# Three reordered steps, no address pads and a few more buffers in a transformer-like block of three token mixers

## The chip, the cores and the metric

The kernel runs on one core of one Trainium2 chip. The metric is the device time of one execution in microseconds; lower is better. All times below are for that one core.

## The reference

One layer over 512 positions of width 1024, all in float32: an RMS norm, one input projection whose columns feed three token mixers and three gates, a merge with an output projection and a residual, and a SwiGLU FFN (inner width 2816) with a second residual.

```python
h = rms_norm(x, norm_mix)
u_pool, u_lru, q, k, v, g_logits = split(h @ w_in)
gates = sigmoid(g_logits + b_gate)                  # three of them
y_pool = pool_mixer(u_pool, w_pool, pool_scale)     # windows 2, 4, 8, 16: mean minus the token, a map per group
y_lru = rglru_mixer(u_lru, ...)                     # see below
y_sb = stick_breaking_attention(rms_norm(q), rms_norm(k), v)   # 8 heads of 128
merged = sum(gates[i] * (y_i @ w_branch[i]))
x = x + merged @ w_out
h2 = rms_norm(x, norm_ffn)
out = x + (silu(h2 @ w_ffn_gate) * (h2 @ w_ffn_up)) @ w_ffn_down

# rglru_mixer
xc = conv_b + sum(conv_w[k] * shifted(u, k))        # width 4, causal
r, i = sigmoid(xb @ w_rg + b_rg), sigmoid(xb @ w_ig + b_ig)    # block-diagonal
log_a = -8 * r * softplus(-lru_lambda)
a, mult = exp(log_a), sqrt(-expm1(2 * log_a))
h = scan(h_prev * a + mult * (i * xc))
```

## The kernel before, in words

**Numbers.** Every float32 product is made from two reduced-precision parts: an operand is split into a high part (ScalarE copies it to the matmul's type) and a low part (VectorE subtracts the high part from the original), and three matmuls are done, high by high, high by low and low by high. A weight tile is 128 partitions by 1024 values. `split_w` and `split_a` do the splits; the tiles `whi` and `wlo` come from a rotation of three buffers each, which `weight_tiles` hands out.

**Products.** Half of the products (`mm3`, `chan_chunk`) are plain, with 512 columns per matmul. The others (q, k, v, the third branch's gates and projection, most of the FFN) use a seven-product scheme of block matrices: the blocks "11", "12", "S2", "S1", "S3", "S4", "22" are sums and differences of quarter matrices. Most of these have 256 columns per matmul.

**Order.** The program is written out by hand, with one long list of weight tiles (`specs`) that `weights()` fetches, loads and splits ahead of use. Background work stands in lists (`bg`, `abg`); `tick()` takes one item off between groups of matmuls, and `step()` appends one. A scheduler then orders each engine's instructions by priority (earlier in the program is higher; `tc.high_priority(n)` raises it by n) and by when buffers and operands are ready. Each engine works through its own order strictly.

**Stages.** (1) The input norm and the first two branches' gates. (2) The recurrence in four chunks of 256 channels: `lru_chunk` does the projection, `conv`, `split` (`xch`, `xcl`) and the gates' matmuls `lg` with tanh on ScalarE; then `lru_exp`, `lru_decay`, `lru_input`, `lru_scan`, `lru_store`. `lru_exp` takes the exponentials in place in `r` and the square root of `t` into a new tile `ls`; `lru_decay` overwrites `t`. (3) The seven-products for v, k, q (tiles `ps_q`), then the third branch's gates (`ps_gx`, `ps_gy`, in two blocks `cc`), stored to DRAM. (4) The pooling mixer in four chunks (`pool_chunk`, in the order of `POOL`) with the attention heads as background. `evac_u` copies a finished pooling bank to a work buffer `up`, and `pool_mean` and `pool_back` go on from there. (5) The plain branch projections (`ps_br`) with loads of gates (`g`). (6) The third branch (`ps_bY`, `ps_bX`), the output projection (`ps_out`), the second norm. (7) The FFN: two chunks of 256 inner channels are plain ("direct", `ps_fg` and `ps_fu`, then `sg` and `act`), nine are seven-products (`seven(c)`, tiles `ps_y`, `ps_x`), and the down product (`ps_dy`, `ps_dx`) ends it.

**Buffers.** In the first stages the pool `ap0` has buffers of 4 KB per partition under three tags: "w" (8, for weights of the seven-products), "t" (8) and "b" (13). In the mixer stage `slot` hands out work buffers of 2 KB (NSP - NLD = 30) and `slot_ld` load buffers (NLD = 12), into which SyncE's queue loads three tiles `at` for each attention head and two gate tiles `g` for each chunk of a branch. `gp` in the FFN has GBUFS = 27 buffers.

**Pads.** `weight_tiles` makes tiles of 1024 + 128 values and uses 1024 of them from offset `o`. It is 0 in the plain products; in the seven-products of 256 columns the first four tiles of a stage take 0, 4, 8 and 12 (STEPS) and all later ones 16 (OFF). One more tile, `pad`, of 41 values stands near the start of memory.

Of the kernel before, what the change touches and what calls it, by code (L numbers as in the profile page):

```python
# [16 lines left out]
P = 128  # L17
# [11 lines left out]
GBUFS = 27  # L29
# [5 lines left out]
PAD = 41  # L35


OFF = 16
STEPS = (0, 4, 8, 12)
NAW, NAT, NAB = 8, 8, 13  # L40
NSP = 42
# [26 lines left out]
def layer_kernel(ctx: ExitStack, tc: tile.TileContext, x, xt, vecs, w_in, w_qkv7, w_gate7, w_pool, w_rg, w_ig,  # L68
# [65 lines left out]
    def split_w(raw, shape, n, o=0):  # L134
        hi, lo = weight_tiles("whi" + n, "wlo" + n, o)
        if len(shape) == 3:
            hi, lo = (t.rearrange("p (a b) -> p a b", a=shape[1]) for t in (hi, lo))
        else:
            hi, lo = (t.rearrange("p (a b c) -> p a b c", a=shape[1], b=shape[2]) for t in (hi, lo))
        with tc.high_priority(60):  # L140
            act(hi, raw, AF.Copy)  # L141
            dve.tensor_tensor(lo, raw, hi.bitcast(F32), ALU.subtract)  # L142
        return hi, lo
# [58 lines left out]
    def add_seven(un, nm, i):  # L202
        u, pieces, shape = UNITS[un]
        last = i == pieces - 1

        def make(n):
            if nm == "S4":
                r = qraw[u, "12", i]
                dve.tensor_tensor(r, r, qraw[u, "S2", i], ALU.add)
            src = qraw[u, {"S1": "21", "S3": "11", "S4": "12"}.get(nm, nm), i]  # L210
            o = 0
            if u >= 3:
                o = goffs.pop(0) if goffs else OFF
            parts = split_w(src, [P] + list(shape), n, o)
# [12 lines left out]
    goffs = list(STEPS)  # L227

# [29 lines left out]
    boffs = list(STEPS)  # L258
# [4 lines left out]
    def add_branch7(u, nm):  # L263
        def make(n):
# [5 lines left out]
            parts = split_w(t, [P, 2, 4, P], n, boffs.pop(0) if boffs else OFF)  # L270
# [58 lines left out]

    cst.tile([P, PAD], F32, tag="pad", name="pad")  # L330
    warm = cst.tile([P, S], BF16, tag="warm", name="warm")
# [109 lines left out]
    with ExitStack() as first:  # L441
# [12 lines left out]
        for i in range(WARM):  # L454
            nc.tensor.matmul(wps[:, 0, :], warm[:, 0:P], warm, start=True, stop=True)
# [233 lines left out]
        def lru_exp(cs):  # L689
            for c in cs:  # L690
                for j in range(2):
                    r = lru[c]["r"][:, j, :]
                    ct = 2 * c + j
                    act(r, r, AF.Exp, scale=cneg[:, ct:ct + 1], bias=cneg[:, ct:ct + 1])
            for c in cs:
                lru[c]["s"] = b4([2, S], f"ls{c}")
                act(lru[c]["s"], lru[c]["t"], AF.Sqrt, scale=0.25)


        def lru_decay(c):  # L700
            e, t = lru[c]["r"], lru[c]["t"]
            dve.scalar_tensor_tensor(t, e, 1.0, t, ALU.add, ALU.mult)
            if c < 2:
                dve.tensor_scalar(t, t, -1.0, 1.0, ALU.mult, ALU.add)
            else:
                act(t, t, AF.Identity, scale=-1.0, bias=1.0)

        def lru_input(c):
            e, s_ = lru[c]["r"], lru[c]["s"]
# [3 lines left out]
        def lru_scan(c):  # L713
            t, s_ = lru[c]["t"], lru[c]["s"]
# [62 lines left out]
        for f, c in ((lru_decay, 2), (lru_decay, 3), (lru_input, 2)):  # L777
            step(of(f, c))
# [112 lines left out]
        for cc in range(2):  # L891
            tx, ty = b4([2, S], f"gx{cc}"), b4([2, S], f"gy{cc}")
# [49 lines left out]
    with ExitStack() as mix:  # L942
# [35 lines left out]
        def evac_u(ps, name):  # L978
            u = slot(name)
            act(two(u), in_order(ps), AF.Copy)  # L980
# [314 lines left out]
    with ExitStack() as ffn:  # L1295
# [115 lines left out]
        offs = []  # L1411
# [14 lines left out]
        def make_a(upto):  # L1426
            while made[0] < min(upto, len(steps)):
                c, nm = steps[made[0]]
                made[0] += 1
                if (c, nm) == (NDIRECT, "11"):  # L1430
                    offs.extend(STEPS)
# [6 lines left out]
        def split_a(src, n):  # L1438
            o = offs.pop(0) if offs else OFF
            h, l = (t.rearrange("p (w k c) -> p w k c", w=2, k=4)  # L1440
                    for t in weight_tiles("wh" + n, "wl" + n, o))
# [35 lines left out]
        def seven(c):  # L1477
# [13 lines left out]
            for n, (nm, ps, half, first, t, ts_, src, ss) in enumerate(plan):  # L1491
# [8 lines left out]
                if nm == "22":  # L1500
                    finish_act(ty, Y, a[:, 1, :])
            acts.append(a)

        bg.extend([lambda: None, rms2] + prepare_b())
        for c in range(NDIRECT):
# [5 lines left out]
            for j in range(2):  # L1511
# [4 lines left out]
                dve.tensor_tensor(a[:, j, :], sg, rb2, ALU.mult)  # L1516
            acts.append(a)
        tick(len(bg))
        for c in range(NDIRECT, NF // 2):
# [49 lines left out]
        def make_d(upto):  # L1569
            while dmade[0] < min(upto, len(dsets)):  # L1570
                nm, n = dsets[dmade[0]]
                dmade[0] += 1
                if dmade[0] == 1:
                    offs.extend(STEPS)
# [157 lines left out]
```

## Time and profile before

| | us |
|---|---|
| median of 3 runs | 872.93 (872.79 to 872.95) |
| the profiled execution, its own time | 872.6 |
| its span from first to last instruction | 870.8 |
| TensorE busy | 859.7 |
| VectorE busy | 741.2 |
| ScalarE busy | 522.1 |
| granted TensorE clock, mean | 1.00 |

In the profile PE is TensorE's matmuls, PEld its weight loads, DVE is VectorE, ACT ScalarE, POOL GpSimd and SP SyncE; L123 is a line of the kernel before. A row of a timeline gives start, duration, engine, line, operation, the tile written and the tiles read, and in brackets how long the engine stood idle before it and what ended that. The end of a matmul is modelled, so two matmuls are compared by their starts. A row of the chain that ended last gives the start, the length and the work.

### The profile page before, as it was taken

How to read it: one execution, taken by the hardware profiler on the slowest of the kernel's cores; microseconds unless marked ns; L12 is line 12 of the kernel's file. 1: busy time of each engine (PE TensorE's matmuls, PEld its weight loads, DVE VectorE, ACT ScalarE, POOL GpSimd, SP SyncE). 2: the span in 40 equal slices, each digit the busy share in tenths (PEclk: the TensorE clock that was granted, in tenths of full speed). 3: DMA queues.
4: the chain of work that ended last, by engine and by line, in shares of the span. 5: the costliest groups of instructions: out<-in, count | busy, mean ns of one | idle time of the engine just before them, and what ended most of it. 6: DMA issues, size and time to landing. Idle time of an engine off the chain costs nothing.

```text
span 870.8 us, 14268 instructions
## 1 busy us (share of the span) xinstructions
PE 859.7 (99%) x5563; PEld 789.7 (91%) x5563; DVE 741.2 (85%) x961; ACT 522.1 (60%) x727; POOL 91.8 (11%) x130
## 2 busy tenths in 40 slices
PE   9999999999999999999999999999999999999998
PEld 7888878888899888889889998889999999999998
DVE  7899897998787699977898786699988888899974
ACT  6554989556856565565665545464555555755642
POOL 1110002232433101000001100000000000121200
PEclk9999999999999999999999999999999999999999
DMA  9686356799582786635736955345543343798913
GB/s 340 167 291 195 97 169 194 215 318 253 176 271 73 238 246 205 218 122 155 217 98 152 212 171 170 98 138 151 150 117 97 106 114 109 233 243 204 192 39 121
DMA packets 116643, 154.08 MB, mean 177 GB/s; under 512 B 8160, under 2 KB 90080, under 8 KB 116576
## 3 DMA queue, kind: packets, MB, share of 16 engines
q1 hardware_dynamic: 103904, 107.30, 38.5%
q0 software_dynamic: 12528, 45.62, 22.1%
q8 instruction: 43, 0.70, 0.3%
q10 hardware_dynamic: 144, 0.26, 0.1%
q14 instruction: 24, 0.20, 0.1%
HBM read 132.71 MB, written 18.87 MB: 174 GB/s over the span
## 4 chain that ended last, share of the span: by engine, by line
PE 76%; DVE 10%; ACT 6%; DMA 4%; issue 2%; SPq 1%; POOL 0%; ACTq 0%; DVEq 0%; POOLq 0%
PE ps_y L318 10%; PE ps_x L318 8%; PE ps_q L834 6%; PE ps_dy L1651 6%; PE ps_dx L1651 5%; DVE wlo L142 3%; PE ps_br L309 3%; PE ps_br L310 3%; PE ps_br L311 3%; PE ps_bY L1277 2%; PE ps_gate L737 2%; DMA qw<-in_w_gate_dram 2%; PE ps_bX L1277 2%; ACT whi L141 2%; PE ps_gy L318 2%
## 5 line engine op out<-in xcount | busy, mean ns | idle before, releaser
L141 ACT ACTIVATE whi<-raw 128x1024 fp32r<-128x1024 f32 x69 | 72.8, 1055 | 76.8 <-PE ps_out L310 16.0
L142 DVE TENSOR_TENSOR wlo<-raw,whi 128x1024 fp32r<-128x1024 f32 x69 | 84.2, 1220 | 23.6 <-ACT whi L141 23.0
L142 DVE TENSOR_TENSOR wlo<-qw,whi 128x1024 fp32r<-128x1024 f32 x48 | 58.4, 1219 | 17.3 <-ACT whi L141 17.1
L141 ACT ACTIVATE whi<-qw 128x1024 fp32r<-128x1024 f32 x48 | 50.4, 1052 | 29.9 <-PE ps_q L834 14.9
L1442 ACT ACTIVATE wh_S<-w_S 128x1024 fp32r<-128x1024 f32 x36 | 38.0, 1059 | 33.0 <-PE ps_y L318 19.9
L1555 POOL DMA_DIRECT2D dw<-in_w_down_dram x20 | 16.9, 862 | 306.3 <-DMA dw<-in_w_down_dram 263.8
L1443 DVE TENSOR_TENSOR wl_S<-w_S,wh_S 128x1024 fp32r<-128x1024 f32 x36 | 43.7, 1220 | 3.8 <-ACT wh_S L1442 3.8
L1442 ACT ACTIVATE wh<-w 128x1024 fp32r<-128x1024 f32 x27 | 28.6, 1058 | 26.9 <-issue 9.1
L1443 DVE TENSOR_TENSOR wl<-w,wh 128x1024 fp32r<-128x1024 f32 x27 | 32.9, 1220 | 8.4 <-ACT wh L1442 8.4
L1442 ACT ACTIVATE whdS<-dw 128x1024 fp32r<-128x1024 f32 x20 | 21.2, 1058 | 21.3 <-PE ps_dy L1651 10.6
L1443 DVE TENSOR_TENSOR wldS<-dw,whdS 128x1024 fp32r<-128x1024 f32 x20 | 24.2, 1220 | 5.5 <-ACT whdS L1442 5.5
L1093 DVE TENSOR_TENSOR_SCAN E<-K,ahead 128x512 f32<-128x512 f32 (+3 forms) x32 | 25.3, 812 | 3.9 <-ACT K L1089 3.9
L309 PE MATMUL ps_br<-yHH,whi 128*128 128x512 f32 x64 | 24.6, 385 | 1.4 <-ACT up L980 1.4
L309 PE MATMUL ps_lru<-HH,whi 128*128 128x512 f32 x64 | 24.6, 384 | 0.0
L309 PE MATMUL ps_br<-yph,whi 128*128 128x512 f32 x64 | 24.5, 383 | 0.0
L309 PE MATMUL ps_pool<-HH,whi 128*128 128x512 f32 x64 | 24.5, 383 | 0.0
L309 PE MATMUL ps_gate<-HH,whi 128*128 128x512 f32 x64 | 24.4, 381 | 0.0
L310 PE MATMUL ps_br<-ypl,whi 128*128 128x512 f32 x64 | 24.3, 379 | 0.0
L311 PE MATMUL ps_gate<-HH,wlo 128*128 128x512 f32 x64 | 24.3, 379 | 0.0
L310 PE MATMUL ps_gate<-HL,whi 128*128 128x512 f32 x64 | 24.3, 379 | 0.0
L310 PE MATMUL ps_br<-yHL,whi 128*128 128x512 f32 x64 | 24.3, 379 | 0.0
L311 PE MATMUL ps_br<-yHH,wlo 128*128 128x512 f32 x64 | 24.3, 379 | 0.0
(740 smaller groups left out, 3444.1 us busy)
## 6 DMA issues: line engine op xcount, KB each, us to landing
raw<-in_w_in_dram SPq DMA_DIRECT2D x31, 512.0 KB, 5.1
qw<-in_w_qkv_dram SPq DMA_DIRECT2D x24, 512.0 KB, 7.0
dw<-in_w_down_dram POOLq DMA_DIRECT2D x20, 512.0 KB, 7.6
w<-in_w_ffn_gate_dram SPq DMA_DIRECT2D x36, 256.0 KB, 3.6
w<-in_w_ffn_up_dram SPq DMA_DIRECT2D x36, 256.0 KB, 4.5
raw<-in_w_branch_dram SPq DMA_DIRECT2D x16, 512.0 KB, 3.9
qw<-in_w_qkv_dram POOLq DMA_DIRECT2D x12, 512.0 KB, 8.0
qd<-r POOLq DMA_DIRECT2D x12, 512.0 KB, 7.4
```

What stands on the lines that cost most here:

```text
L141: act(hi, raw, AF.Copy)
L142: dve.tensor_tensor(lo, raw, hi.bitcast(F32), ALU.subtract)
L309: nc.tensor.matmul(ps, lh, rh, start=start, stop=False, skip_group_check=skip)
L310: nc.tensor.matmul(ps, lh, rl, start=False, stop=False, skip_group_check=skip)
L311: nc.tensor.matmul(ps, ll, rh, start=False, stop=stop, skip_group_check=skip)
L318: nc.tensor.matmul(o, a_[a][:, w, k, :], il2(b_[b][:, k, :]), start=first and n == k == 0, stop=last and n == 2 and k == 3, skip_group_che ...
L834: nc.tensor.matmul(ps[:, a, :], b_[:, k, ts_], il(a_[:, kk, :]), start=first and n == k == 0, stop=n == 2 and k == 3, skip_group_check=True)
L1093: dve.tensor_tensor_scan(E[:, c0:c0 + n][:, ::-1], K[:, c0 + 1:c0 + n + 1][:, ::-1], ahead[:, S - n:][:, ::-1], 0.0, ALU.mult, ALU.add)
L1277: nc.tensor.matmul(o, ah[x_][:, w, k, :], il2(b[k][y_]), start=first_ and n == k == 0, stop=n == 2 and k == 3, skip_group_check=True)
L1442: act(h, src, AF.Copy)
L1443: dve.tensor_tensor(l, src, h.bitcast(F32), ALU.subtract)
L1651: nc.tensor.matmul(o, a_[a][:, w, k0 + k, :], il2(b_[b][:, k, :]), start=first and i == k == 0, stop=last and i == 2 and k == nk - 1, skip ...
```

## The change

Three things move. In the recurrence the square root is taken out of `lru_exp` into `lru_root`, which works in place in `t`; `lru_decay` writes a new tile `a`, and comes before the root. The copies of the last pooling chunk go to load buffers, at high priority. The element-wise work on the second direct FFN chunk is put after the products "12" and "S2" of the first seven-product chunk.

The offsets and the pad go. The tile of ones for the warm-up matmuls shrinks from 512 to 128 columns, read four times. There are more buffers: "b" 14 instead of 13, work buffers 32 instead of 30 (NSP 44), GBUFS 28 instead of 27. The tiles of the second block of third-branch gates lie in "w" buffers instead of "b".

```diff
-GBUFS = 27
+GBUFS = 28
...
-PAD = 41
-OFF = 16
-STEPS = (0, 4, 8, 12)
-NAW, NAT, NAB = 8, 8, 13
-NSP = 42
+NAW, NAT, NAB = 8, 8, 14
+NSP = 44
...
-    def weight_tiles(nh, nl, o=0):
-        return [wp.tile([P, 1024 + 128], F32R, tag=tag, name=n)[:, o:o + 1024]
+    def weight_tiles(nh, nl):
+        return [wp.tile([P, 1024], F32R, tag=tag, name=n)
                 for tag, n in (("whi", nh), ("wlo", nl))]
...
-    cst.tile([P, PAD], F32, tag="pad", name="pad")
-    warm = cst.tile([P, S], BF16, tag="warm", name="warm")
+    warm = cst.tile([P, P], BF16, tag="warm", name="warm")
...
-            nc.tensor.matmul(wps[:, 0, :], warm[:, 0:P], warm, start=True, stop=True)
+            nc.tensor.matmul(wps[:, 0, :], warm, warm.unsqueeze(1).to_broadcast([P, 4, P]), start=True, stop=True)
...
+        def lru_root(cs):
             for c in cs:
-                lru[c]["s"] = b4([2, S], f"ls{c}")
-                act(lru[c]["s"], lru[c]["t"], AF.Sqrt, scale=0.25)
+                act(lru[c]["t"], lru[c]["t"], AF.Sqrt, scale=0.25)

         def lru_decay(c):
             e, t = lru[c]["r"], lru[c]["t"]
-            dve.scalar_tensor_tensor(t, e, 1.0, t, ALU.add, ALU.mult)
+            a = lru[c]["a"] = b4([2, S], f"la{c}")
+            dve.scalar_tensor_tensor(a, e, 1.0, t, ALU.add, ALU.mult)
...
-        step(of(lru_exp, (0,))), step(c2), step(s2), step(g1)
+        step(of(lru_exp, (0,)), of(lru_decay, 0), of(lru_root, (0,))), step(c2), step(s2), step(g1)
         gate1(0)
-        step(of(lru_decay, 0), t1), step(of(lru_exp, (1,))), step(g2), step(of(lru_input, 0))
+        step(t1), step(of(lru_exp, (1,)), of(lru_decay, 1), of(lru_root, (1,))), step(g2), step(of(lru_input, 0))
...
-        step(c3), step(s3), step(of(lru_decay, 1), of(lru_scan, 0)), step(t2, of(lru_input, 1))
+        step(c3), step(s3), step(of(lru_scan, 0)), step(t2, of(lru_input, 1))
...
-        for f, c in ((lru_decay, 2), (lru_decay, 3), (lru_input, 2)):
-            step(of(f, c))
+        step(of(lru_decay, 2), of(lru_decay, 3)), step(of(lru_root, (2, 3))), step(of(lru_input, 2))
...
-            tx, ty = b4([2, S], f"gx{cc}"), b4([2, S], f"gy{cc}")
+            tx, ty = (b4([2, S], f"g{n}{cc}", "bw"[cc]) for n in "xy")
...
-        def evac_u(ps, name):
-            u = slot(name)
-            act(two(u), in_order(ps), AF.Copy)
+        def evac_u(ps, name, last):
+            u = (slot_ld if last else slot)(name)
+            with tc.high_priority(EARLY if last else 0):
+                act(two(u), in_order(ps), AF.Copy)
             return u
...
-            us = [evac_u(pss[j], f"up{g}{j}") for j in range(2)]
+            us = [evac_u(pss[j], f"up{g}{j}", g == POOL[3]) for j in range(2)]
...
+                if (c, n) in after:
+                    after[c, n]()
...
-            for j in range(2):
+            def direct_act(j, c=c, a=a, pg=pg, pu=pu):
                 sg = small(f"sg{c}{j}", 2, "sq2")
                 dve.tensor_tensor(two(sg), in_order(pg[j]), two(rb2), ALU.mult)
                 act(sg, sg, AF.Silu)
                 dve.tensor_tensor(two(sg), two(sg), in_order(pu[j]), ALU.mult)
                 dve.tensor_tensor(a[:, j, :], sg, rb2, ALU.mult)
+
+            if c < NDIRECT - 1:
+                direct_act(0), direct_act(1)
             acts.append(a)
         tick(len(bg))
+        after = {(NDIRECT, 1): lambda: direct_act(0), (NDIRECT, 2): lambda: direct_act(1)}
```

The users of the offsets (the third branch's gates and projection, the FFN and the down product) lose their lists of offsets.

More of the change, by code (lines that the diff above doesn't have):

```diff
@@ L127, in halves, with split_w @@
         return [t[:, 0:2, :], t[:, 2:4, :]]
-    def weight_tiles(nh, nl, o=0):
-        return [wp.tile([P, 1024 + 128], F32R, tag=tag, name=n)[:, o:o + 1024]
+    def weight_tiles(nh, nl):
+        return [wp.tile([P, 1024], F32R, tag=tag, name=n)
                 for tag, n in (("whi", nh), ("wlo", nl))]
-    def split_w(raw, shape, n, o=0):
-        hi, lo = weight_tiles("whi" + n, "wlo" + n, o)
+    def split_w(raw, shape, n):
+        hi, lo = weight_tiles("whi" + n, "wlo" + n)
         if len(shape) == 3:
@@ L210, in make @@
             src = qraw[u, {"S1": "21", "S3": "11", "S4": "12"}.get(nm, nm), i]
[L211 to L214, printed above, removed]
+            parts = split_w(src, [P] + list(shape), n)
             if nm == "11":
@@ L269, in make @@
                 t = (BY if nm in ("11", "S3") else BX)[u]
[L270 removed]
+            parts = split_w(t, [P, 2, 4, P], n)
             if nm in BNEXT:
@@ L713, in lru_scan @@
         def lru_scan(c):
-            t, s_ = lru[c]["t"], lru[c]["s"]
+            t, s_ = lru[c]["a"], lru[c]["t"]
             h = lru[c]["i"]
@@ L1438, in split_a @@
         def split_a(src, n):
-            o = offs.pop(0) if offs else OFF
             h, l = (t.rearrange("p (w k c) -> p w k c", w=2, k=4)
-                    for t in weight_tiles("wh" + n, "wl" + n, o))
+                    for t in weight_tiles("wh" + n, "wl" + n))
             act(h, src, AF.Copy)
```

13 lines of the change are left out of this document (3 added, 10 removed).

## The prediction

> **What bounds the kernel now.** I read the page first (busy times, then the chain that ended last), then TensorE's own timeline wherever it stood still, then VectorE's and ScalarE's timelines at those places.
>
> ```profile
> PE 859.7 (99%) x5563; PEld 789.7 (91%) x5563; DVE 741.2 (85%) x961; ACT 522.1 (60%) x727; POOL 91.8 (11%) x130
> PE 76%; DVE 10%; ACT 6%; DMA 4%; issue 2%; SPq 1%; POOL 0%; ACTq 0%; DVEq 0%; POOLq 0%
> ```
>
> TensorE is busy for 859.7 of 870.8 us, so at most about 11 us can come out of any change that leaves the matmuls alone, and this one does. The chain leaves TensorE for VectorE and ScalarE in only 16% of the span: these are the places where a split weight or a copied bank came late. What counts is the start-to-start time of two matmuls around a stop.
>
> ```profile
> 120.31 0.48 PE L664 MATMUL lg<-xch,lwh 64*128 64x512 f32 x2
> 122.13 0.48 PE L664 MATMUL lg<-xcl,lwh 64*128 64x512 f32 x2 [1.33 <-DVE xcl L654]
> ...
> 144.23 0.38 PE L834 MATMUL ps_q<-whi,HH 128*128 128x512 f32 x1
> 144.83 0.48 PE L834 MATMUL ps_q<-wlo,HH 128*128 128x512 f32 x1 [0.21 <-DVE wlo L142]
> ...
> 149.90 0.38 PE L834 MATMUL ps_q<-whi,hT2h 128*128 128x512 f32 x1
> 150.50 0.48 PE L834 MATMUL ps_q<-wlo,hT2h 128*128 128x512 f32 x1 [0.23 <-DVE wlo L142]
> ...
> 160.75 0.38 PE L834 MATMUL ps_q<-whi,hT3h 128*128 128x512 f32 x1
> 161.81 0.48 PE L834 MATMUL ps_q<-wlo,hT3h 128*128 128x512 f32 x1 [0.68 <-DVE wlo L142]
> ...
> 347.74 0.38 PE L310 MATMUL ps_br<-yHL,whi 128*128 128x512 f32 x1
> 347.96 0.38 PE L311 MATMUL ps_br<-yHH,wlo 128*128 128x512 f32 x1
> 349.77 0.48 PE L309 MATMUL ps_br<-yHH,whi 128*128 128x512 f32 x1 [1.43 <-ACT up L980]
> ...
> 600.89 0.28 PE L318 MATMUL ps_y<-B0T2l,wh_S 128*128 128x256 f32 x1
> 601.00 0.28 PE L318 MATMUL ps_y<-B0T2h,wl_S 128*128 128x256 f32 x1
> 601.40 0.38 PE L318 MATMUL ps_x<-B0T1h,wh_S 128*128 128x256 f32 x1
> 601.61 0.28 PE L318 MATMUL ps_x<-B0T1l,wh_S 128*128 128x256 f32 x1
> 602.66 0.38 PE L318 MATMUL ps_x<-B0T1h,wl_S 128*128 128x256 f32 x1 [0.77 <-DVE wl_S L1443]
> ```
>
> In full flow a 512-column matmul starts 0.22 us after the last (347.74 to 347.96), a 256-column one 0.11 us (600.89 to 601.00). Less that, the stops are: 1.60 us in the recurrence (120.31 to 122.13); 0.38, 0.38 and 0.84 us, together 1.60, in the first of the three q/k/v products; 1.59 us after the last pooling chunk (347.96 to 349.77); and 0.29 and 0.94 us, together 1.23, in the first seven-product chunk of the FFN. The sum is 6.0 us. The three reorderings aim at these four places.
>
> **Root in place.** Before, `lru_decay` overwrites `t`, which the square root reads, so VectorE must wait until ScalarE has done the exponentials, loaded a table and taken the root.
>
> ```profile
> 103.56 1.51 ACT L694 ACTIVATE lr<-lr,cneg 128x512 f32<-128x512 f32 x2
> 105.09 1.28 ACT L697 ACT_TABLE_LOAD   x1
> 106.39 1.06 ACT L697 ACTIVATE ls<-lt 128x1024 f32<-128x1024 f32 x1
> ...
> 107.47 1.23 DVE L702 SCALAR_TENSOR_TENSOR lt<-lr,lt 128x1024 f32<-128x1024 f32 x1 [2.36 <-ACT ls L697]
> ...
> 132.74 2.92 ACT L694 ACTIVATE lr<-lr,cneg 128x512 f32<-128x512 f32 x4
> ...
> 136.64 1.22 DVE L142 TENSOR_TENSOR wlo<-qw,whi 128x1024 fp32r<-128x1024 f32 x1 [2.54 <-ACT whi L141]
> 139.01 1.23 DVE L702 SCALAR_TENSOR_TENSOR lt<-lr,lt 128x1024 f32<-128x1024 f32 x1 [1.15 <-ACT ls L697]
> ```
>
> The decay of chunk 1 stood 2.36 us, and everything behind it in VectorE's order stood too: the convolution and the split of chunk 3, whose `xcl` TensorE then waits for at 122.13. After the change the decay writes a new buffer `a` and needs only the exponentials, which end at 105.07; it can run beside the table load, 105.1 to 106.3, and the root behind it, which now overwrites `t` and so waits for the decay, need not start before 106.39 anyway. Operations, shapes and counts stay (1.23 us for the decay, 1.06 for the root), and `a` takes the one buffer that the root's output took. The 2.36 us are more than the stop of 1.60, so I take all of it: **-1.6**. Queued behind the new wait on ScalarE are the weight split and the gates' tanh; in this case the wait costs them nothing.
>
> The decays of chunks 2 and 3 likewise lose the wait for the root (1.15 us). Their exponentials end at 135.66 (132.74 + 2.92), the first pair of them half-way, and VectorE stands 2.54 us for a weight up to 136.64; so one or both decays can move there, up to 2.5 us earlier for all splits of the q/k/v product. This could remove the whole 1.60. But the third and longest stop (0.84) lies 20 us later, and work of low priority can be put before that split again. Ends 0 and 1.6; I take half: **-0.8**. The roots of 2 and 3 now come in a step of their own, so their table load can fall among the gates' tanh; the price is under rival 2.
>
> **Last pooling copies.** Their source is complete when the last pooling matmul is done (343.43 + 0.38), yet they run at 349.10:
>
> ```profile
> 343.43 0.38 PE L311 MATMUL ps_pool<-HH,wlo 128*128 128x512 f32 x1
> ...
> 344.34 0.63 ACT L938 ACTIVATE p31h<-up 128x512 fp32r<-128x512 f32 x1 [3.55 <-DVE up L994]
> ...
> 349.10 1.10 ACT L980 ACTIVATE up<-ps_pool 128x512 f32<-128x512 f32 x2
> ```
>
> ScalarE was idle for 3.55 us before 344.34, and the copies came last of all at 349.10, after operations emitted later: as I read it they had no work buffer (30 of them, with the pooling of the chunk before, attention and split weights in them). With two of the 12 load buffers and high priority the first copy can run as its half completes, the second at about 344, both inside the idle time, and TensorE finds its bank at 348. Two more work buffers (32) push the same way. I take the whole stop: **-1.6**. The price lies on SP: the copies hold two load buffers for some 20 us, and the attention's and gates' loads behind them rotate through ten.
>
> ```profile
> at<-qd SPq DMA_DIRECT2D x24, 256.0 KB, 5.7
> ```
>
> An `at` load that waits for a buffer holds every weight load queued behind it on SP. Ends: nothing, while loads run a head ahead; 5.7 us (one landing in full) if one comes just in time. Nearer to nothing, since four heads' loads fit today: **+0.4**.
>
> **Direct FFN chunk later.** Its six VectorE operations run among the first splits of the seven-product:
>
> ```profile
> 593.69 0.68 DVE L1513 TENSOR_TENSOR sg<-ps_fg,rb 128x512 f32<-128x512 f32 x1
> ...
> 600.17 0.68 DVE L1516 TENSOR_TENSOR act<-sg,rb 128x512 f32<-128x512 f32 x1
> 601.38 2.36 DVE L1443 TENSOR_TENSOR wl_S<-w_S,wh_S 128x1024 fp32r<-128x1024 f32 x2 [0.52 <-ACT wh_S L1442]
> ...
> 610.74 5.36 PE ps_y L318 x48
> ```
>
> Six of 0.68 us, overlapping a little, are some 3.6 us ahead of the split that TensorE waits for at 602.66. Emitted after the "12" and "S2" products they come behind the splits of S1 and S3, and the stop of 1.23 goes. But VectorE has little free time here (the 0.52 us in front of that split), and the same 3.6 us now stand ahead of the splits of S4 and 22, so part comes back there. Ends 0 and 1.23, and I take **-0.9**. The banks of the gate and up products are held some 5 us longer; the chunk that reuses them starts with the second half of the last row, at 613.4, so that costs nothing.
>
> **Warm-up, buffers, gates.** The shorter memset of `warm` starts the nine warm matmuls up to some tenths earlier; they stay nine. It brings nothing, since the first real matmul waits for its data:
>
> ```profile
> 5.28 0.73 PEld L737 LDWEIGHTS ps_gate<-hu,whi 128*128 128x128 f32 x4 [0.71 <-ACT hu L470]
> ```
>
> The last gates' two tiles lie in weights' buffers that the gate weights of the block before have left; their stores on POOL stay where they are. Between -0.5 and +0.5 (as the smallest stops above), taken as 0, like the buffers NAB 14 and GBUFS 28.
>
> **No pads.** Weight tiles lose their shift of 0, 4, 8, 12, then 16 floats, and everything behind the pad moves. One stage goes through all five shifts:
>
> ```profile
> 471.63 2.68 PE ps_bY L1277 x24
> 474.31 5.36 PE ps_bX L1277 x48
> ...
> 482.35 2.68 PE ps_bX L1277 x24
> ```
>
> The first tile (471.63) is shifted by 0, the next two by 4 and 8, the one at 482.35 by 16: 2.68 us for 24 matmuls each time. Rounding hides at most 0.4 ns of 112 per matmul; over some 3,024 of these (counted from the code: 7 tiles of 24 in two gate blocks, two branch blocks and nine FFN chunks, and 840 in the down product) that is 1.2 us either way. I take 0.
>
> **Sum.** -1.6 - 0.8 - 1.6 + 0.4 - 0.9 = -4.5 us. The profiled run took 872.6 us (span 870.8 and 1.8 around it), 0.3 below the median of 872.93; so 868.4 for the median. If everything falls and more of the small waits go with it, about 865.
>
> **Rivals.** Rival 1, the gain moves instead of going: VectorE is 85% busy, and the splits that were late by 0.4 to 0.8 us become late a few microseconds on; the load buffers cost one landing (5.7 us) against the 4.9 of the rest. For it speaks VectorE almost without a gap in the FFN; against it that both idle times of 2.36 and 3.55 us are real and are used. Time 873.7 at most, within 0.2% of 872.9 (about what a measurement of this kernel can tell from no change, 1.75 us).
>
> Rival 2, slower: the root waits among the gates' tanh.
>
> ```profile
> 92.37 1.28 ACT L668 ACT_TABLE_LOAD   x1
> 93.66 0.68 ACT L668 ACTIVATE lr<-lg,brg 64x512 f32<-64x512 f32 x1
> ...
> 96.40 1.22 DVE L702 SCALAR_TENSOR_TENSOR lt<-lr,lt 128x1024 f32<-128x1024 f32 x1
> ```
>
> Chunk 0's root ran before 92 in ScalarE's slack, but its decay came only at 96.40. If the decay stays there, root and two table loads (1.28 + 1.06 + 1.28 = 3.6 us) fall into the tanh run from 93.66 on, and the convolution gates behind them are late by that. For two chunks that is 7.2 us; with the recurrence's and the product's gain gone and only pooling and FFN left (-1.6 - 0.9), +4.7: 877.6. It decides from 4.25 us of new TensorE waiting on (1.75 more than these 2.5). Against it: ScalarE is 60% busy, and decay and root can both come before 94.
> The Trainium skill, "ScalarE: Activation LUTs", sections "Table sets: the hidden batching unit" and "What ACT_TABLE_LOAD costs", speaks against the change: group by table set, all exponentials and then all roots, since a switch costs about 2.66 us, load and drain. By that figure, an estimate, the rival's two roots would cost 12.8 us and it would end at 883. The trace has the load at 1.28 us with the next activation 0.02 us after it (106.39), so the lower price stands above.
>
> Rival 3, the addresses matter after all: 1 ns on each of the 3,024 matmuls is 3.0 us; from 2.1 ns (4.5 + 1.75 us) it is slower. The rows above speak against it, for shifts of 0, 4, 8 and 16; only the pad's move of all other tiles isn't in them.
>
> **How the numbers follow.** Forecast 0.64 (865.0 to 871.2), rival 1 0.17 (871.2 to 874.7), rival 2 0.13, rival 3 0.06. So faster 0.64, same 0.17, slower 0.19. The range of 865.0 to 874.7 leaves out rivals 2 and 3.
>
> **What would show it.** Right: the decay of chunk 1 without a wait for `ls`, no stop before `xcl` of chunk 3; `up` of the last chunk near 344 and no stop of `ps_br`; `sg` of the second direct chunk after the S1 split, and no stop at S1. Wrong: the root behind a wait for VectorE with tanh between two table loads, `pq` waiting for `at`, or 24 matmuls of 256 columns off 2.68 us.

## The result, and the profile after

The changed kernel takes 874.76 us (median of 18 runs, 872.88 to 876.52), the kernel before 872.82 (18 runs, 871.75 to 873.71): ratio 1.002, interval 1.0013 to 1.0026. It is slower by 1.9 us; 4.5 us less was forecast. The profiled execution after took 875.74 us, with a span of 874.0 and a mean granted clock of 0.998.

The page of the kernel after, busy times and the shares of the chain that ended last:

```profile
PE 862.2 (99%) x5563; PEld 790.5 (90%) x5563; DVE 741.3 (85%) x961; ACT 521.9 (60%) x727; POOL 90.9 (10%) x130
PE 80%; ACT 7%; DVE 7%; DMA 4%; issue 2%; POOL 0%; SPq 0%; ACTq 0%; DVEq 0%; POOLq 0%
```

Every engine does the same work; only its places differ. So the answer lies again in the stops, by the starts of two matmuls less 0.22 us (0.11 with 256 columns).

**Recurrence.** The root of chunk 0 in ScalarE's timeline, before and then after:

```profile
90.35 1.06 ACT L697 ACTIVATE ls<-lt 128x1024 f32<-128x1024 f32 x1
```

```profile
92.13 1.28 ACT L688 ACT_TABLE_LOAD   x1
95.70 1.06 ACT L688 ACTIVATE lt<-lt 128x1024 f32<-128x1024 f32 x1 [2.30 <-DVE la L694]
96.78 1.28 ACT L658 ACT_TABLE_LOAD   x1
98.08 0.68 ACT L658 ACTIVATE lr<-lg,brg 64x512 f32<-64x512 f32 x1
```

VectorE's timeline after, ahead of that decay and around the idle time at 105, and TensorE's:

```profile
92.18 1.22 DVE L139 TENSOR_TENSOR wlo<-raw,whi 128x1024 fp32r<-128x1024 f32 x1
93.31 1.22 DVE L663 SCALAR_TENSOR_TENSOR li<-li,xc 128x1024 f32<-128x1024 f32 x1
94.45 1.22 DVE L694 SCALAR_TENSOR_TENSOR la<-lr,lt 128x1024 f32<-128x1024 f32 x1
...
108.30 1.23 DVE L139 TENSOR_TENSOR wlo<-raw,whi 128x1024 fp32r<-128x1024 f32 x1 [2.41 <-ACT whi L138]
```

```profile
103.47 0.38 PE L302 MATMUL ps_lru<-HH,wlo 128*128 128x512 f32 x1
104.68 0.48 PE L654 MATMUL lg<-xch,lwh 64*128 64x512 f32 x2 [0.83 <-ACT li L659]
...
122.41 0.48 PE L654 MATMUL lg<-xch,lwh 64*128 64x512 f32 x2
122.73 0.38 PE L654 MATMUL lg<-xcl,lwh 64*128 64x512 f32 x2
```

Before, the root of chunk 0 followed its exponentials in ScalarE's slack. Now ScalarE has the table loaded at 93.41 (92.13 + 1.28) and then waits 2.30 us for the decay, which VectorE reaches at 94.45. The tanh behind it start at 98.08, where they started at 93.66 before. TensorE waits for them: 0.26 us at 101.39, 0.99 at 103.47 and 0.39 at 116.42. The stop of 1.60 in front of `xcl` is gone, and these are 1.64 together. And VectorE's idle time at 105 is still there, 2.41 us instead of 2.36; its end now bears the name of `whi` instead of `ls`.

**q/k/v.** TensorE's and ScalarE's timelines:

```profile
147.30 0.38 PE L825 MATMUL ps_q<-whi,HL 128*128 128x512 f32 x1
148.44 0.48 PE L825 MATMUL ps_q<-whi,HH 128*128 128x512 f32 x1 [0.76 <-ACT whi L138]
150.70 0.48 PE L825 MATMUL ps_q<-wlo,HH 128*128 128x512 f32 x1 [1.78 <-DVE wlo L139]
...
151.46 0.63 PE L825 MATMUL ps_q<-wlo,HH 128*128 128x512 f32 x1
...
154.45 0.58 PE L825 MATMUL ps_q<-whi,HL 128*128 128x512 f32 x1
154.86 0.38 PE L825 MATMUL ps_q<-whi,hT2h 128*128 128x512 f32 x1
```

```profile
144.40 1.04 ACT L688 ACTIVATE lt<-lt 128x1024 f32<-128x1024 f32 x1
145.46 1.28 ACT L596 ACT_TABLE_LOAD   x1
146.75 0.69 ACT L596 ACTIVATE gt<-ps_gate,bhalf 128x512 f32<-128x512 f32 x1
147.34 1.05 ACT L138 ACTIVATE whi<-qw 128x1024 fp32r<-128x1024 f32 x1
```

The stops are 0.92 and 2.04, together 2.96 where they were 1.60. Behind them eight matmuls, from 151.46 on, start 0.43 us apart instead of 0.22: another 1.7 us in this execution (the last section has the clock that goes with them).

**Pooling.** TensorE's and VectorE's timelines; the copies `up` were at 342.18 and 349.86:

```profile
359.04 0.38 PE L302 MATMUL ps_br<-yHH,wlo 128*128 128x512 f32 x1
360.93 0.79 PE L1048 MATMUL pq<-idn,at 128*128 128x128 f32 x5 [1.51 <-DVE wtl L1101]
```

```profile
356.87 0.68 DVE L981 TENSOR_TENSOR pw<-up 128x511 f32<-128x511 f32 x1
...
359.06 1.22 DVE L139 TENSOR_TENSOR wlo<-raw,whi 128x1024 fp32r<-128x1024 f32 x1
360.19 1.15 DVE L1101 TENSOR_TENSOR wtl<-pw,wth 128x512 fp32r<-128x512 f32 x2
```

No `ps_br` matmul stands around 348 any more, but TensorE stands 1.67 us at 359.04, for the low part `wtl`, which has `pool_mean`'s sums in front of it. The second copy came 2.1 us after its source was complete (347.41 + 0.38), not at once, and was still in time.

**FFN.** TensorE's timeline at the place of the old stops:

```profile
605.21 0.28 PE L309 MATMUL ps_x<-B0T1h,wh_S 128*128 128x256 f32 x1
605.33 0.28 PE L309 MATMUL ps_x<-B0T1l,wh_S 128*128 128x256 f32 x1
...
607.78 0.28 PE L309 MATMUL ps_x<-B0T1h,wl_S 128*128 128x256 f32 x1
608.25 0.38 PE L309 MATMUL ps_y<-B0T3h,wh_S 128*128 128x256 f32 x1 [0.20 <-ACT tx L1483]
```

The 1.23 us are gone; 0.36 come at 607.78, in front of the product S3 and for ScalarE's copy `tx`, not for a split.

The account of the profiled runs: recurrence 0.04 (1.64 less 1.60), q/k/v 1.36 and 1.7, pooling 0.08 and another 0.34 at 366.5, a gate product at 261 to 265 0.3 (0.95 less 0.66), FFN -0.87: 3.0 of the 3.2 us between the spans.

### The profile page after: what moved, and what is told of

It is laid out like the page before. It is cut to its first block, busy times and chain, and to the rows that moved or that the text cites. A ratio compares the mean times of both kernels' runs of the same rounds, so it can differ in the third digit from the quotient of the medians.

```text
span 874.0 us, 14262 instructions
## 1 busy us (share of the span) xinstructions
PE 862.2 (99%) x5563; PEld 790.5 (90%) x5563; DVE 741.3 (85%) x961; ACT 521.9 (60%) x727; POOL 90.9 (10%) x130
## 4 chain that ended last, share of the span: by engine, by line
PE 80%; ACT 7%; DVE 7%; DMA 4%; issue 2%; POOL 0%; SPq 0%; ACTq 0%; DVEq 0%; POOLq 0%
PE ps_y L309 11%; PE ps_x L309 8%; PE ps_q L825 7%; PE ps_dy L1644 6%; PE ps_dx L1644 5%; PE ps_br L301 2%; PE ps_br L300 2%; PE ps_bY L1269 2%; PE ps_br L302 2%; PE ps_gate L729 2%; DMA qw<-in_w_gate_dram 2%; PE ps_gy L309 2%; PE ps_bX L1269 2%; ACT whi L138 2%; DVE wlo L139 2%
## 5 line engine op out<-in xcount | busy, mean ns | idle before, releaser
L302 PE MATMUL ps_lru<-HH,wlo 128*128 128x512 f32 x64 | 24.4, 381 | 0.0
L301 PE MATMUL ps_lru<-HL,whi 128*128 128x512 f32 x64 | 24.3, 379 | 0.0
L301 PE MATMUL ps_pool<-HL,whi 128*128 128x512 f32 x64 | 24.3, 379 | 0.0
```

Source lines behind the costliest of these rows:

```text
L301: nc.tensor.matmul(ps, lh, rl, start=False, stop=False, skip_group_check=skip)
L302: nc.tensor.matmul(ps, ll, rh, start=False, stop=stop, skip_group_check=skip)
```

## The experiments

Each ratio is against the kernel before, run on the same chip beside it; 1 us is 0.0011 in the ratio.

### One part alone

Each part of the diff by itself on the kernel before: the new root, decay and order of steps; `evac_u` with `slot_ld`; `direct_act`; all the rest.

> Only the root's move (decay into a new tile, root in place behind it, steps in the new order), with everything else as before. Theory A (the root's move lost time: the root of chunk 0 waits for its decay and stands among the gates' tanh, those of chunks 2 and 3 hold up the splits of the q/k/v product, and the stop there lowers the granted clock for some microseconds): slower than before by 2.5 to 4.5 us, about 876; the stop before xcl of chunk 3 gone, new ones behind lg and ps_gate, 3 us around 147 to 151, granted clock of the span 0.998. Theory B (the loss comes from the pads, the addresses or the buffers, and the root's move is worth what was forecast): faster by 1.6 to 2.4, about 871.

> Only the last pooling copies in load buffers at high priority; the rest as before. Theory A (the stop only moves: the last pool_mean stands ahead of the low part that the first branch needs): the stop of 1.6 us at 348 gone, one of about 1.7 at 359 in its place, time within 0.5 us of before. Theory B (the copies alone are worth 1.6, and the stop at 359 comes from the other parts): 1.2 to 1.6 faster, no stop over 0.5 us between 345 and 365.

> Only the second direct FFN chunk's element-wise work put later; the rest as before. Theory A (this part does what was forecast): faster by 0.9 to 1.0 us, about 871.9, no stops at 598 to 603 and one of 0.36 us near 608. Theory B (the stops come back later in the seven-products): within 0.3 us of before.

> Only the pads and offsets taken out, one more buffer in two places and two more work buffers, the smaller warm-up tile and the last gates in weights' buffers; all three orders as before. Theory A (these are worth nothing): within 0.5 us of before, 24 matmuls of 256 columns still 2.68 us. Theory B (the addresses or the fuller buffers cost time): slower by 2 to 3 us, with the groups of 24 matmuls above 2.68 us or new waits for buffers.

| alone | median, us | ratio |
|---|---|---|
| root | 875.25 | 1.0026 (1.0016 to 1.0035) |
| pooling copies | 873.26 | 1.0004 (0.9995 to 1.0013) |
| FFN | 871.69 | 0.9991 (0.9982 to 1.0000) |
| rest | 872.79 | 0.9994 (0.9985 to 1.0003) |

The four add to +1.8 us (2.45 + 0.46 - 1.11 - 0.01 from the median of before beside them, 872.80); the whole change makes +1.9. The root is the loss; the FFN part is the only gain, and its interval ends at no change. All four came out nearest to their theory A, the root at the lower edge of it (2.45 us of the 2.5 to 4.5 expected). The root's part alone has the whole change's stops in its profiled run, 0.91 and 2.04 in the q/k/v product, and 1.50 at the gate product (0.66 before), but no slower matmuls behind them. The pooling copies alone have the same picture as the whole, in TensorE's and VectorE's timeline:

```profile
355.18 0.38 PE L311 MATMUL ps_br<-yHH,wlo 128*128 128x512 f32 x1
356.04 1.61 DVE L1110 TENSOR_TENSOR wtl<-pw,wth 128x512 fp32r<-128x512 f32 x3
...
356.78 1.12 PE L1057 MATMUL pq<-idn,at 128*128 128x128 f32 x8 [1.22 <-DVE wtl L1110]
```

1.38 us at 355.18 and 0.33 a little later, for the 1.59 that went. Before, VectorE reached the same splits at nearly the same time, and TensorE did not have to wait for them, being behind by its stop at 348:

```profile
355.71 1.61 DVE L1109 TENSOR_TENSOR wtl<-pw,wth 128x512 fp32r<-128x512 f32 x3
```

### Which chunk's root

```diff
 # against the kernel before; e7: root in place, decay into a new tile and new steps for c < 2 only
+                lru[c]["s"] = lru[c]["t"] if c < 2 else b4([2, S], f"ls{c}")
...
+            a = lru[c]["a"] = b4([2, S], f"la{c}") if c < 2 else t
 # e14: for c >= 2 only; e17: for c == 0 only
```

> Root's move for chunks 0 and 1 only; chunks 2 and 3 take their roots and decays as before. Theory A (the loss lies in the q/k/v product, by the late roots of 2 and 3, the recurrence only swaps one stop of 1.6 for three of 1.65 together): within 0.5 us of before, about 872.9, stops at 101, 103 and 116 as with the whole move, and at 144 to 161 as before. Theory B (both halves lose): 874 or more.

> Root's move for chunks 2 and 3 only (decay into a new tile, root in place behind it in a later step); chunks 0 and 1 as before. Theory A (the q/k/v stops grow by what chunks 0 and 1 hand on): recurrence as before (1.6 at 120), q/k/v stops 1 to 2 us in all, within 0.6 us of before: 872.4 to 873.6. Theory B (the late roots of 2 and 3, behind the gates' tanh with two table loads, hold up the high parts): q/k/v stops of 3 us or more in all, 874.3 to 876.

> Root's move for chunk 0 only (decay into a new tile, root in place behind it); chunks 1, 2 and 3 as before. Theory A (chunk 0 is the cost: its root waits on ScalarE for a decay that VectorE reaches late, and the tanh behind it start 4.4 us later): 1.8 to 3 us slower than before, 875 to 876, ScalarE idle over 2 us in front of the root at 92 to 96 and stops behind lg at 101 to 104. Theory B (chunk 1's move is the cost): within 0.6 us of before, 872.4 to 873.6.

Chunks 0 and 1: 875.74, 1.0032 (1.0021 to 1.0043). Chunks 2 and 3: 873.05, 0.9999 (0.9990 to 1.0008). Chunk 0 alone: 877.35, 1.0041 (1.0028 to 1.0054). The expectation of the first, that the loss lies with 2 and 3, was wrong: chunk 0 is the loss, and its 3.9 us are more than the 1.8 to 3 expected. By the medians, moving 1 as well mends part of it; the two intervals overlap, and chunk 1's move without chunk 0's was not run. With 2 and 3 alone the q/k/v stops are 0.76 and 0.31, less than the 1.60 before. With 2 and 3 as before and only chunk 0 moved they are 3.41 together, with 0 and 1 moved 3.94. ScalarE's, VectorE's and TensorE's timelines with chunk 0 alone:

```profile
96.61 1.07 ACT L699 ACTIVATE lt<-lt 128x1024 f32<-128x1024 f32 x1 [2.30 <-DVE la L705]
```

```profile
112.98 1.23 DVE L705 SCALAR_TENSOR_TENSOR lt<-lr,lt 128x1024 f32<-128x1024 f32 x1 [2.54 <-ACT ls L699]
...
144.20 1.23 DVE L705 SCALAR_TENSOR_TENSOR lt<-lr,lt 128x1024 f32<-128x1024 f32 x1 [3.77 <-ACT ls L699]
```

```profile
152.28 0.38 PE L836 MATMUL ps_q<-whi,HL 128*128 128x512 f32 x1
154.97 0.48 PE L836 MATMUL ps_q<-whi,hT2h 128*128 128x512 f32 x1 [2.30 <-ACT r L849]
```

ScalarE, some 4 us late behind that root, starts the exponentials of chunks 2 and 3 at 138.88 instead of 132.74 (this profiled run began its recurrence 1.0 us later than that of before). It hands the delay to VectorE: 2.54 us at the next root, after 2.42 for `whi` (before, 2.36 in all), and 3.77 at the roots of 2 and 3 (before, 1.15 there and 2.54 ahead of it for `whi`). And TensorE gets it 50 us later: 2.47 us at 152.28, for a bank that ScalarE has yet to copy.

### The wait, or the order

```diff
 # against the changed kernel
 # e5: without the pooling copies; the decay writes la, the root its own ls in lru_exp as before; steps as before
 # e6: the new steps, but the root writes its own ls
-                act(lru[c]["t"], lru[c]["t"], AF.Sqrt, scale=0.25)
+                lru[c]["s"] = b4([2, S], f"ls{c}")
+                act(lru[c]["s"], lru[c]["t"], AF.Sqrt, scale=0.25)
```

> The change without its pooling copies and with another root: the decay writes a new tile, but the root keeps its own tile and its old place in the exponentials' step, and the steps stand in the old order; so neither waits for the other. The FFN part and the rest are in (-1.1 and 0 by their own runs). Theory A (what cost time was the root's wait for the decay): no 2.3 us of ScalarE in front of a root, tanh of chunk 1 near 94 again, no stops behind lg at 101 to 104, the stop of 1.6 at 120 gone, and the q/k/v stops at most 1.6 in all: 869 to 871. Theory B (VectorE's and ScalarE's order decide, and taking away the wait only moves the stop): recurrence or q/k/v stops again 1.6 or more above that, 871.5 to 874.

> As the run with the root's move alone, but the root writes a tile of its own, as before, so it does not wait for the decay; the new order of the steps stays. Theory A (the wait for the decay is the cost): the stops at 101 to 117 (1.65 us) gone and the one at 148 under 1 us, 3 to 4 us faster than the root's move alone, about 871.5. Theory B (the order of the steps is the cost, with the roots of chunks 2 and 3 and two table loads behind the gates' tanh): within 1 us of the root's move alone, about 874.5 to 875.5. If the wait costs in chunks 0 and 1 and the order in 2 and 3: 1.6 us below it, about 873.6.

e5: 872.43, 0.9995 (0.9986 to 1.0004), no better than FFN and rest make it. The decay no longer waits for the root, but in the order that came out it stands at 122.70; VectorE still stands at 105, since the next operation in its order needs the root too. The stops around 120 are 0.52 and 1.67:

```profile
107.38 1.23 DVE L701 SCALAR_TENSOR_TENSOR ls<-lr,ls 128x1024 f32<-128x1024 f32 x1 [2.10 <-ACT ls L687]
```

e6: 875.68, 1.0031 (1.0019 to 1.0043). The root no longer waits, but it and its two loads (92.50 to 96.14) still stand in front of the tanh, where the kernel before had the root and the first load in ScalarE's slack ahead of 91.4. The exponentials of chunk 1 start at 106.17 instead of 103.56, and VectorE's decay waits for them:

```profile
107.71 1.22 DVE L705 SCALAR_TENSOR_TENSOR la<-lr,lt 128x1024 f32<-128x1024 f32 x1 [2.31 <-ACT lr L694]
```

The recurrence's stops are 0.82 and 1.40, more than the 1.64 with the wait; the q/k/v stops are 0.67 and 0.87, no more than before. (1.6 us of e6's loss are something else: TensorE stands 1.99 us at 301 for a late `at`, where it is 0.37 before; why the load is late there was not followed up. Without these e6 loses some 0.9 us, the time of its third expectation, but not by that one's stops.) In both the wait was taken away and nothing was won in the recurrence: the operation that came next in VectorE's order needed a later link of the same chain on ScalarE, the root in e5 and the exponentials in e6.

### The roots left out

```diff
-                act(lru[c]["s"], lru[c]["t"], AF.Sqrt, scale=0.25)
+                act(lru[c]["s"], lru[c]["t"], AF.Copy if c == 1 else AF.Sqrt, scale=0.25)   # e9, on the kernel before
 # e10: AF.Copy for all, on the kernel before; e11: AF.Copy for all, on the changed kernel
```

> The kernel before, with the square root of chunk 1 left out: a copy of the same shape stands in its place, so the two table loads of 1.28 us around it go (2.56 us of ScalarE) and the decay of chunk 1 still waits for that operation. Theory A (ScalarE's chain of tanh, exponentials and root limits the recurrence from 93 to 108; VectorE's idle of 2.4 us at 105 only bears the name of whatever is next in its order): the idle time shrinks by over 1 us although the decay still waits, and the stop of 1.6 us at 120 goes: 871 to 871.8. Theory B (VectorE's amount of work is the limit there): the stop stays above 1 us, 872.5 to 873.3.

> The kernel before with all four square roots left out (copies of the same shape, no table loads for them). Together with the next run it prices the table loads in the old order and in the new. Theory A (old order hides most of them): 1.5 to 3 us faster than before, 870 to 871.3. Theory B (they cost nothing in the old order): within 0.8 us of before.

> The changed kernel with all four square roots left out (copies of the same shape in place, no table loads for them; each still waits for its decay). Theory A (what the new order of roots cost was root and two table loads among the tanh, and behind the gates): 3.5 to 5 us faster than the changed kernel, 870 to 871.3, as the copies in the old order but for the other parts. Theory B (the wait of the copy for the decay is the cost, not the loads): less than 2 us faster, 872.8 to 874.

e9: 874.26, 1.0018 (1.0009 to 1.0026). VectorE's idle time at 105 fell to 0.94 us as theory A had it, and the stop at 120 to 1.04, but the q/k/v stops became 0.68, 0.71 and 1.94: a miss for both theories. e10: 871.03, 0.9979 (0.9970 to 0.9988), with no stop over 0.2 us left in the recurrence. e11: 873.50, 1.0009 (1.0000 to 1.0017). So without any table load for a root the changed kernel is still 2.5 us behind the old one, although it has the FFN gain in it (and although five of its 11 runs, and none of e10's, have the lower clock of the last section, worth some 0.5 us of this). ScalarE's and TensorE's timelines of e11:

```profile
96.06 1.06 ACT L688 ACTIVATE lt<-lt 128x1024 f32<-128x1024 f32 x1 [3.60 <-DVE la L694]
```

```profile
101.51 0.38 PE L654 MATMUL lg<-xch,lwl 64*128 64x512 f32 x2
103.60 0.48 PE L654 MATMUL lg<-xch,lwh 64*128 64x512 f32 x2 [1.71 <-ACT li L659]
```

The time that the load took becomes waiting for the decay (3.60 instead of 2.30), and TensorE stands 1.87 us at one place where it stood 1.64 at three. So the loads are not what the new order costs in chunk 0. Nor is it the wait alone, for without it (e6) the recurrence's stops are 2.22. What e6 and e11 have in common with the changed kernel is the root's place ahead of the tanh.

### Chunk 1's root out of the chain

```diff
 # e12: FFN part and rest; chunk 1: decay into la, root into ls in a later step
-        step(c3), step(s3), step(of(lru_decay, 1), of(lru_scan, 0)), step(t2, of(lru_input, 1))
+        step(of(lru_decay, 1), c3), step(s3), step(of(lru_scan, 0)), step(t2, of(lru_root, (1,)), of(lru_input, 1))
 # e15: also la for chunks 2 and 3
```

> The FFN part and the rest of the change, without its pooling copies and with another root: chunks 0, 2 and 3 as before; for chunk 1 the decay writes a new tile and so does the root, which stands one group of steps later, behind the tanh of chunk 2. In VectorE's order the convolution of chunk 3 (whose product is ready at 105.1) then follows at once where the idle time was. Theory A (ScalarE's chain was the limit; with root and table loads out of it VectorE fills the 2.4 us): no idle time over 1.2 us at 105 to 108, no stop at 120, q/k/v stops between 1.6 and 2.5: 869.5 to 871. Theory B (the stop comes back whole in the q/k/v product, by VectorE's work that now comes later): stops of 3 us or more from 139 to 165, 871.5 to 873.

> As the run with chunk 1's root later, and the decays of chunks 2 and 3 write new tiles too, so that they need not wait for their roots, whose place stays. Theory A (the decay's wait for the root, 1.8 us of idle VectorE at 137.5, is part of the stop at 142 to 145): q/k/v stops 1.5 or less in all instead of 2.9, 0.8 to 1.5 us faster than that run. Theory B (VectorE's next operation waits for the same ScalarE chain, as in the recurrence): q/k/v stops within 0.7 us of 2.9, same time.

VectorE's and TensorE's timelines of e12:

```profile
104.95 1.53 DVE L629 TENSOR_SCALAR xc<-ps_lru,vt 128x512 f32<-128x512 f32 x2
107.37 1.23 DVE L139 TENSOR_TENSOR wlo<-raw,whi 128x1024 fp32r<-128x1024 f32 x1 [0.89 <-ACT whi L138]
...
117.06 1.22 DVE L644 TENSOR_TENSOR xcl<-xc,xch 128x1024 fp32r<-128x1024 f32 x1
```

```profile
120.22 0.48 PE L654 MATMUL lg<-xch,lwh 64*128 64x512 f32 x2
120.54 0.38 PE L654 MATMUL lg<-xcl,lwh 64*128 64x512 f32 x2
```

Here the convolution of chunk 3 fills the idle time, `xcl` comes 3.8 us earlier (120.86 before) and the stop at 120 is gone. The q/k/v stops are then 0.68, 1.69, 0.22 and 0.33, together 2.92 instead of 1.60, so most of it came back there. e12: 872.25, 0.9989 (0.9980 to 0.9998): 0.8 us faster, no better than its FFN part alone (1.1), and nearer to theory B. e15: 871.53, 0.9985 (0.9976 to 0.9994), with the q/k/v stops of e12 to 0.01 us: the free decays of 2 and 3 are worth nothing there, as theory B had it.

### Pooling

```diff
 # e8 (on e2): one empty step ahead of the last pool_mean
+            bg.extend([lambda: None] * (1 if g == POOL[3] else 0))
 # e13 (on e2): its running sums on GpSimd
+                eng = nc.gpsimd if g == POOL[3] else dve
```

> As the run with the last pooling copies in load buffers alone, but the last chunk's pool_mean is emitted one tick later, so that its six operations of the first half (3 us on VectorE) stand behind the low parts wtl and not ahead of them. Theory A (the copies did remove the stop at 348, and VectorE's pool_mean ahead of wtl gave it back at 355 to 359): the stop of 1.4 us at 355 gone or under 0.5 and none at 348: 1 to 1.6 us faster than the copies alone, about 871.8. Theory B (TensorE waits there for something else, the loads or the head's own chain): time as with the copies alone, 873.2, and a stop of over 1 us between 355 and 360.

> The last pooling copies in load buffers, as in the run with these alone, and the running sums of the last chunk's pool_mean on GpSimd instead of VectorE (some 5 us of VectorE's work in two halves). Theory A (the stop moved to 355 and, with pool_mean later, to 372 because VectorE has more work there than time): with that work off VectorE no stop above 0.5 us from 345 to 375: 1.4 to 2 us faster than the copies alone, about 871.5. Theory B (TensorE waits there for an attention head's own chain, VectorE's load does not matter): a stop of over 1.2 us stays between 355 and 375, time 873 or more (VectorE may even wait for GpSimd).

e8: 875.16, 1.0020 (1.0012 to 1.0029), slower than either theory expected. The stop at 355 went, as theory A had it, and 2.65 us came at 372.64, where VectorE's sums now stand ahead of what TensorE needs:

```profile
372.64 0.28 PE L311 MATMUL z<-qkh,qkl 128*128 128x256 f32 x1
375.40 0.55 PE L1108 MATMUL pw<-idn,A 128*128 128x128 f32 x3 [2.49 <-DVE ypl L1009]
```

e13: 872.56, 0.9997 (0.9987 to 1.0006). With the sums off VectorE the stop at 356.16 is 0.81 instead of 1.38 and none over 0.2 us follows up to 380: theory A's cause, not its size. What was probably in the way stands in the last section.

### Together

> The parts that could help, together: FFN part, the rest, chunk 1's root later, last pooling copies in load buffers with the running sums of the last pool_mean on GpSimd. Theory A (the parts add: 872.2 for the first three, and 1.4 to 2 for the pooling): 870.3 to 870.9, no stops of over 1 us but those from 142 to 145. Theory B (pooling gives nothing, by GpSimd's sums or another stop): 872 to 873.

> The combined version, with the roots and decays of chunks 2 and 3 moved as in the change. Theory A (these two shorten the q/k/v stops as they did alone, from 1.6 to 1.1): q/k/v stops 2.0 to 2.4 instead of 2.9, 869.8 to 870.6. Theory B (with chunk 1's later work in the way the order no longer matters): within 0.5 us of the combined version, 870.6 to 871.5.

e16 (e12 and e13 in one): 871.03, 0.9976 (0.9965 to 0.9987), 0.1 us above theory A's range and 1 below theory B's. e18 (chunks 2 and 3 as in the change besides): 871.24, 0.9977 (0.9968 to 0.9986). Both beat the kernel before by 2.0 to 2.2 us, and the changed one by more; for e18 theory B holds, as its q/k/v stops (0.46, 0.40, 1.24, 0.87 and 0.66) are no smaller than those of e12.

## Why the prediction was wrong, step by step

**Root in place (-1.6, measured about 0 in the recurrence).** Two steps failed. The first: "The 2.36 us are more than the stop of 1.60, so I take all of it". The idle time was read as the price of the wait named in its row. It was the place where VectorE had caught up with ScalarE, whose chain of tanh, exponentials, root and split runs nearly without a gap from 93.66 to 108: with the wait gone the row read `whi` (2.41), the next reader of the root (2.10) or the exponentials (2.31). Another operation moved into the gap (e12) took it down to 0.89 and the stop at 120 away, but the time won there was mostly lost again in the q/k/v product. The second failed step is for chunk 0, which the sum did not cost at all: that "decay and root can both come before 94" stood against rival 2. VectorE was busy until 94.45 with what its order had ahead of the decay (`wlo`, `li`), so the root held ScalarE's tanh. The row that pointed to it was quoted: the decay of chunk 0 at 96.40. Alone, this part was to gain 2.4 us (1.6 and 0.8) and lost 2.45. How much of that is the wait and how much the place ahead of the tanh stays open: e6, without the wait, loses as much, but 1.6 us of it at the late load.

**q/k/v (-0.8).** For its own edit the step had the right sign: with only chunks 2 and 3 moved the stops fell by 0.5 (1.60 to 1.07), too little to be seen in the time (0.9999). In the whole the stops grew by 1.4 (2.96), and 1.7 came by the slower matmuls behind them in the profiled run, because ScalarE arrives late from chunk 0: with that chunk alone moved they are 3.41. That delay had no term.

**Pooling (-1.6 + 0.4, measured +0.5, within its interval of none).** The copies were in time and the stop at 348 went, as forecast. The failed step is "I take the whole stop": nothing was looked for behind it. VectorE's row of operations was the later limit (`wtl` at 355.71 before and at 356.04 with the copies alone), and before, the stop had kept TensorE from meeting it. The price for the load buffers was not seen: in front of the one late `at` TensorE was idle for 0.20 us before (299.92) and 0.19 after (303.91).

**FFN (-0.9, measured -1.1) and rest (0, measured 0.0).** Right in size, by the stops (1.23 to 0.36) and by the runs alone. What came back was to come ahead of the splits of S4 and 22; it came ahead of S3, for `tx`, so this part of the number is luck. The pads are worth nothing that these runs can tell: 24 matmuls of 256 columns still take 2.68 us (475.71 and 483.74 after).

**The rivals.** Rival 2 is what happened, by its mechanism, in chunk 0 as it said, and at a smaller price than 7.2 us: the tanh were 4.4 us later, but TensorE lost only 1.64 us there and 1.4 later, and the stop of 1.60 did go. The Trainium skill, "ScalarE: Activation LUTs", section "What ACT_TABLE_LOAD costs", has 2.66 us for a switch, from which the prediction's estimate of 883 came. The trace does not agree: it has 1.28 us and the next activation 0.02 us behind it (96.78, 98.08). And e11 shows that the order loses even with no load. Rival 1 is what happened in the pooling stage. Of rival 3 nothing was seen.

## What to carry to other kernels

An idle time in a trace is named after the last thing awaited, but belongs to the engine whose chain gets there last: before costing a removed wait, ask when the next operations in the waiting engine's order would be ready, and whether they come from the same chain. A stop of the bound engine that goes is only won if the other engines are ahead of it at the next place. And an in-place write turns a free operation of one engine into a wait for another (here 2.30 us), and what stands behind it in that engine's order starts later too (here the tanh, by 4.4 us).

## What the runs showed of the hardware

**A slower clock behind a stop.** In the profiled run after, eight matmuls from 151.46 to 154.86 ran 0.43 us apart, 3.40 us in all, then at full rate again. In the sums over this stretch the third number from the end is the granted clock, 0.51 of full speed:

```profile
151.40:154.90 3.50, 3.50 (x10) 2.76 (x10) 3.50 (x4) 0.37 (x1) 0.45 (x1) 0.51 0.39 150
```

One such stretch in 874 us makes a mean clock of 0.998. Of the 18 runs 8 have that (mean time 875.45), the other 10 have 1.000 (874.08), and these too are 1.3 us slower than the median of before. The Trainium skill, "TensorE: Matmul & The Clock Gate", section "Part 1: The HAM clock gate", says that the clock is halved after an idle window of about 3.4 us and that the windows run freely; the trace agrees with the half rate, the length of 3.40 us and a difference from run to run, although TensorE was not idle all the time before it (the matmul at 148.44 ran between the two stops). The profiled run of e1 has the same two stops (0.91 and 2.04) and a granted clock of 1.00 behind them, and three of its nine runs have 0.998. Which stops bring it stays open: e8, with a stop of 2.65 us, shows 0.998 in 7 of 11 runs, e17, with one of 2.47, in none of 5, and e5, with none over 1.67 in its profile, 0.998 or less in 5 of 12.

**GpSimd and VectorE hold each other up.** VectorE's and GpSimd's timelines of e13:

```profile
347.00 1.76 DVE L1069 TENSOR_TENSOR vl<-at,vh 128x512 fp32r<-128x512 f32 x1 [0.31 <-ACT vh L1068]
```

```profile
347.13 1.07 POOL L991 TENSOR_TENSOR pw<-up 128x511 f32<-128x511 f32 x1
...
348.77 2.02 POOL L991 TENSOR_TENSOR pw<-pw 128x510 f32<-128x510 f32 x1
```

`vl` takes 0.69 us elsewhere (349.99 in the kernel after is one), here 1.76: its own 0.69 and the 1.07 of the sum on GpSimd. The sum at 348.77 takes 2.02 beside a split on VectorE of 1.21. The Trainium skill, "SBUF — State Buffer", section "SBUF: two separate sides", says that a VectorE operation with two inputs in SBUF and a GpSimd operation that reads SBUF shut each other out: the one that starts first has the port for its whole length. The lengths agree; the order does not, as far as the rows tell, since `vl` is the one that got longer and is shown starting 0.13 us ahead of the sum. This is the likely reason that taking the sums off VectorE won 0.6 us there and not the whole stop; that was not tried by itself.
